# A hybrid attention and expert layer on one core: the last GpSimd work ahead of the experts is moved to VectorE, the gate vector's sums are moved later, and one hook of the experts one block on

## The chip, the cores and the metric

One core of one Trainium2 chip runs the whole layer in a single launch. The metric is the device time of the launch in microseconds (us), lower is better. The engines are named as in the profile: PE is TensorE, PEld its weight loads, DVE VectorE, ACT ScalarE, POOL GpSimd, SP SyncE. SP, POOL and ACT also issue DMA transfers.

## The reference

For 512 latent tokens of width 1024 (and 256 context tokens that are only read):

- A modulation vector is made from `c` with `w_ada`; its six parts of 1024 are shift, scale and gate of the attention half and of the expert half. The last part is the gate vector `g_m`.
- Two attention branches (grouped-query and differential) are computed, projected, merged with gates, and multiplied with `w_out`; `x = x + g_a * (...)`.
- `h = rmsnorm(x) * (1 + sc_m) + sh_m`. A router `h @ router_w + router_b` picks the top 4 of 32 experts for each token, with a softmax over the four.
- Each expert is `((up + 1) * gate * sigmoid(1.702 gate)) @ w_down + b_down` with clamped gate and up; `x = x + g_m * (weighted sum over the four)`.

All is in float32. Each expert has three weight matrices of 1024 x 1024, 4 MB each, so the experts read 403 MB.

## The kernel before

The code is written in program order, and a scheduler of the language may move instructions on each engine, except inside a `manual_schedule` block, where the engines that it lists keep the written order.

**Up to the experts.** After the attention, `out_products` multiplies with `w_oa` and `w_ob`, then the output projection with `w_out` runs as two column halves `n` by four token tiles `i`. After the second half of a tile, `x1[i]` is complete and the tile is routed: `scaled` multiplies it with the scale vector into `h2` (two halves of 128x512, on POOL), `routed` makes the reciprocal root `r`, completes `h2` on DVE and writes it to `h2d` in memory by DMA, and leaves three closures that are called later: `transposes`, `logits` (PE product with the router's weights, `lg`, the four largest `m`, the masks `gt`, `eq`, `mkb`) and `ranks` (how many earlier tokens chose the same expert, `rkm`). The product `py` has one PSUM buffer, so the logits of a tile wait until the ranks of the tile before have been read.

For tiles 2 and 3 all this is one chain with nothing else to do on PE: masks of tile 2, ranks, logits of tile 3, masks, ranks, then `one_hot` and `placed` (which tokens go to expert 0, their indices `ix`), then `gathered` (an indirect DMA that reads the rows of `h2d` into `xg`, issued by POOL), then the transposes of `xg` and the first expert's first product. Meanwhile the experts are sorted by their counts; that ends with `rkms` and `auxs`.

**Weights of the experts.** They come in 96 x 4 blocks of 1 MB (`fetch`), into 13 buffers; a block is fetched when a buffer is free (`used_up`). Blocks 8 to 11 are issued by POOL, the others by SP. Experts come in pairs: a large one (128 rows, three float32r products of split operands: `wh` is the rounded weight made by ACT, `wl` the rest, made by `wl = raw - wh`) and a small one (64 rows, plain float32, reading the raw block). `ahead(n)` makes up to `n` splits in advance; the kernel calls `ahead(3)` once before the experts. The subtractions of the first four splits were POOL's, all others DVE's.

**In the experts**, `product` goes through eight blocks `k` of 128 rows and calls the hooks that are given for a `k` first. `down(l, {1: input_of(l + 2), 4: act_of(l + 1)})` is the large expert's down product with two hooks: at `k` = 1 the next input is transposed, at `k` = 4 the small expert's activation `gS` is transposed; both through the one PSUM buffer `pt`. `aS`, its copy, is what the small expert's down product reads.

**The gate vector.** `ada_end` sums a vector's partial products over the 128 partitions: for each half of 512 one product with a matrix of ones and one ACT copy. `gm_bc` (tile `gm`) is first read when expert 0's output is scaled.

Of the kernel before, what the change touches and what calls it, by code (L numbers as in the profile page):

```python
# [8 lines left out]
FT = mybir.dt.float32  # L9
# [9 lines left out]
T, TC, D, E = 512, 256, 1024, 32  # L19
# [13 lines left out]
def tile_hybrid_block(  # L33
# [6 lines left out]
    PE, ACT, DVE, POOL, SP = nc.tensor, nc.scalar, nc.vector, nc.gpsimd, nc.sync  # L40
# [71 lines left out]
    acc = [acc2[:, j] for j in range(2)]  # L112
# [566 lines left out]
    def ada_end(p, a, scale):  # L679
        for n in range(2):  # L680
            ns = slice(n * 512, (n + 1) * 512)
            mm(p[:, ns], ones_f, a[:, ns], True, True)
            ACT.activation(a[:, ns], p[:, ns], AF.Copy, scale=scale)
# [205 lines left out]
            next(fill, None)  # L889
    opened["yp"] = open_pool("yp2", "right", stack=yst)  # L890
    yBH, yBL = halves("yB", yB, DVE)
    for a, scale in ((acc[0], 0.5), (acc[1], 1.0), (gm_bc, 1.0)):
        ada_end(ps.tile([128, D], FT, name="S", bufs=2), a, scale)


# [68 lines left out]
    for g in range(4):  # L964
        DVE.tensor_copy(diag[32 * g:32 * g + 32], marks[32 * g:32 * g + 32, 0, 32 * g:32 * g + 32])

    def expert_bias(j):
        b = braw[32 * j:32 * j + 32]
        if j == 1:
            DVE.tensor_scalar(b, b, 1.0, None, op0=OP.add)  # L970
        o = 64 * (j % 2)
        ACT.copy(bias[o:o + 32, j // 2], b)
        DVE.tensor_sub(bias[o + 32:o + 64, j // 2], b, bias[o:o + 32, j // 2])
# [4 lines left out]
    h2s, hTs = {}, {}  # L978
# [13 lines left out]
    def channels_x1(i, n):  # L992
        if n == 0:
            hTs[i] = fp.tile([128, NK, 128], FT, name="hT", bufs=2)
        pt = ps.tile([128, NK, 128], FT, name="pt", bufs=1)
        for k in range(4 * n, 4 * n + 4):
            PE.transpose(pt[:, k], x1[i][:, k * 128:(k + 1) * 128], ident)
        ACT.copy(hTs[i][:, 4 * n:4 * n + 4], pt[:, 4 * n:4 * n + 4])

    def scaled(i, n):  # L1000
        if n == 0:
            h2s[i] = fp.tile([128, D], FT, name="h2", bufs=2)
        ns = slice(n * 512, (n + 1) * 512)
        POOL.tensor_mul(h2s[i][:, ns], x1[i][:, ns], sc_bc[:, ns])

    def routed(i):

# [62 lines left out]
    for n in range(2):  # L1070
        ns = slice(n * 512, (n + 1) * 512)
        for i in range(4):
            p = ps.tile([128, D], FT, name=("pg", "pu")[i % 2], bufs=1)[:, ns]
            if n:
                channels_x1(i, 0)
            for k in range(NK):
                if n and i and k == 4:
                    stages[i - 1][0]()
                    if i > 1:
                        stages[i - 2][2]()  # L1080
                wh, wl = ws[k // 2][0][:, k % 2], ws[k // 2][1][:, k % 2]
                h, l = (t[k // 4][:, k % 4, i * 128:(i + 1) * 128] for t in (mTH, mTL))
                product3(p, h, l, wh, wl, k == 0, k == NK - 1)
            if n == 0 and i == 0:
                ada_end(ps.tile([128, D], FT, name="py", bufs=1), acc[2], 1.0)
                DVE.scalar_tensor_tensor(sc_bc, sc_bc, 1.0, nm, op0=OP.add, op1=OP.mult)
            if n == 0 and i == 3:
                ws = out_group(1)
            t = fp.tile([128, 512], FT, name="xt", bufs=2)
            DVE.tensor_mul(t, p, ga_bc[:, ns])  # L1090
            DVE.tensor_add(x1[i][:, ns], x1[i][:, ns], t)
            ACT.activation(t, x1[i][:, ns], AF.Square, scale=1.0 / 32.0, accum_out=sqs[:, i, n:n + 1])
            if n:
                scaled(i, 0)
                scaled(i, 1)
                stages.append(routed(i))
                if i:
                    stages[i - 1][1]()
            else:
                if i:  # L1100
                    expert_bias(i - 1)
                if i == 2:
                    router_weights()
# [47 lines left out]
    def ahead(n=BEFORE):  # L1151

        while len(split) < n and at_split[0] < len(to_split):
            i, a = to_split[at_split[0]]
            if i not in raws:
                return
            wh = xp.tile([128, D], FR, name="wh", bufs=BEFORE + 1)
            ACT.copy(wh, raws[i][:, a])  # L1158
            wl = xp.tile([128, D], FR, name="wl", bufs=BEFORE)
            (DVE if at_split[0] > 3 else POOL).tensor_sub(wl, raws[i][:, a], wh)  # L1160
            split[i, a] = wh, wl
            at_split[0] += 1
            if a:
                used_up(i)

    place, xg = {}, []
    for b, n in enumerate((D, 512)):
        t = xp.tile([128, n], FT, name=f"xg{b}")
        POOL.memset(t, 0.0)
        xg.append(t)  # L1170
    with tc.high_priority(300):
        stages[3][0]()
        stages[2][2]()
# [3 lines left out]
    def one_hot(e):  # L1177

        oh = xp.tile([128, 4, 128], FR if e else FT, name="oh", bufs=1)
        r, small = seq[e]  # L1180
        of = (rkms[:, :, r:r + 1] if e else rkm[:, :, 0:1]).to_broadcast([128, 4, 128])
        DVE.tensor_tensor(oh, rep(slots2 if small else slots1, 4), of, op=OP.is_equal)
        return oh

    def placed(e, oh):

        r, small = seq[e]
        pi = ps.tile([128, NK, 128], FT, name="pt", bufs=1)[:, 0, 0:4]
        ix = xp.tile([128, 1], I32, name="ix", bufs=6)
        w = xp.tile([128, 1], FT, name="wsl", bufs=6)  # L1190
        for i in range(4):
            mm(pi if e else pi[:, 0:2], oh[:, i], auxs[:, i, r] if e else aux[:, :, i, 0], i == 0, i == 3)
        if small:
            DVE.scalar_tensor_tensor(ix, pi[:, 0:1], 2.0, none, op0=OP.mult, op1=OP.add)
        else:
            DVE.tensor_scalar(ix, pi[:, 0:1], float(T), None, op0=OP.add)
        if e:
            DVE.reduce_sum(w, pi[:, 1:3], axis=AX)
        else:
            DVE.tensor_copy(w, pi[:, 1:2])  # L1200
        place[e] = ix, w
# [4 lines left out]
    def gathered(e):  # L1206
# [3 lines left out]
            in_offset=bass.IndirectOffsetOnAxis(ap=place[e][0][:, 0:1], axis=0),  # L1210
            bounds_check=(2 * T if small else T) - 1, oob_is_err=False)

    placed(0, one_hot(0))
    gathered(0)
    fetch(2)
    ahead(3)


    srt = ps.tile([128, D], FT, name="py", bufs=1)
# [30 lines left out]
    DVE.tensor_copy(bye, srt[:, 512:768].rearrange("p (a t) -> p a t", a=2))  # L1250
    for a in range(2):
        mm(srt[:, 768 + 128 * a:896 + 128 * a], bye[:, a], blocks.rearrange("p g e -> p (g e)"), True, True)
    DVE.tensor_copy(rkms, srt[:, 768:896].rearrange("p (i e) -> p i e", i=4))
    weights = srt[:, 896:1024].rearrange("p (i e) -> p i e", i=4)
    DVE.tensor_copy(auxs[:, :, :, 1], weights)
    DVE.tensor_sub(auxs[:, :, :, 2], weights, auxs[:, :, :, 1])
    for u in range(2):
        POOL.tensor_add(halvesr[:, u], blocks[:, 2 * u], blocks[:, 2 * u + 1])
    f1.close()


# [101 lines left out]
    def down(e, hooks={}):  # L1363
        p = result(e, 2)
        product(p, A[e], w_down, e, hooks)
        small = seq[e][1]
        y = ep.tile([128, p.shape[1]], FT, name=name_of(e))
        DVE.scalar_tensor_tensor(y, p, place[e][1], gm2 if small else gm_bc, op0=OP.mult, op1=OP.mult)
        POOL.indirect_dma_start(  # L1369
            out=by_place(out2, small), out_offset=bass.IndirectOffsetOnAxis(ap=place[e][0][:, 0:1], axis=0),  # L1370
            in_=y, in_offset=None, bounds_check=(2 * T if small else T) - 1, oob_is_err=False, compute_op=OP.add)

    def input_of(e):
        if e < E:
            X[e] = transposed(xg[e % 2], seq[e][1], "x")

    def act_of(e):
        A[e] = transposed(G[e], seq[e][1], "a")
# [29 lines left out]
    with tc.manual_schedule(engines={mybir.EngineType.PE, mybir.EngineType.Activation, mybir.EngineType.DVE}):  # L1408
        input_of(0)
        gate(0, {1: lambda: hot(1), 4: lambda: place_of(1)})  # L1410
        up(0, {2: lambda: hot(2), 3: lambda: input_of(1), 5: lambda: place_of(2)})
        gate(1, {1: lambda: hot(3), 3: lambda: place_of(3), 5: lambda: act_of(0)})
        up(1, {4: places_counted})
        down(0, {1: lambda: input_of(2), 4: lambda: act_of(1)})
        down(1, {3: lambda: input_of(3)})
        for l in range(2, E, 2):
            gate(l, {0: lambda: hot(l + 2), 3: lambda: place_of(l + 2), 4: lambda: hot(l + 3), 7: lambda: place_of(l + 3)})
            gate(l + 1)
            up(l)
            up(l + 1, {5: lambda: act_of(l)})  # L1420
            down(l, {1: lambda: input_of(l + 2), 4: lambda: act_of(l + 1)})
            down(l + 1, {3: lambda: input_of(l + 3)})
    ex.close()
    right.close()
# [126 lines left out]
```

## Time and profile before

| | us |
|---|---|
| median of three runs | 1627.09 (1625.44 to 1629.03) |
| the profiled execution | 1623.81 |
| its span in the trace | 1621.9 |
| PE busy in the span | 1537.2 (95%) |
| DVE busy | 1056.4 (65%) |
| POOL busy | 222.0 (14%) |

The span is what the trace covers; the 1.9 us beside it lie before the first and behind the last instruction. The median of the runs is 3.3 us above the profiled execution. Busy shares are means over stages with different limits, so the stages around the change are read one by one.

### The profile page before, as it was taken

To read this page: it belongs to the slowest core of one execution; us is meant where nothing else is said; L and a number is where in the kernel's file an instruction comes from. 1 tells how busy PE (TensorE), PEld (TensorE's weight loads), DVE (VectorE), ACT (ScalarE), POOL (GpSimd) and SP (SyncE) were. 2 spreads that over 40 slices of the span, in tenths; PEclk is the share of its full clock that TensorE was granted. 3 is DMA by queue.
4 is the path that set the end of the run, shared out by engine and by line. 5 is a ranking of instruction groups with operands and counts; after the bars stand their busy time and mean duration, and the time that the engine had idled before them with its cause. 6 is when DMAs were issued, how large, how long until landed. Compare 5 with 4: busy or idle time off the path is not lost. (4 is left out here: it accounts for less than half of the span.)

```text
span 1621.9 us, 20787 instructions
## 1 busy us (share of the span) xinstructions
PE 1537.2 (95%) x7303; PEld 1047.6 (65%) x7303; DVE 1056.4 (65%) x1668; ACT 754.1 (46%) x1051; POOL 222.0 (14%) x209
## 2 busy tenths in 40 slices
PE   7999999989999689999999999999999999999997
PEld 2778877778877564666666665656666565566564
DVE  6888888756877865566566575564565655656654
ACT  5668834256633243354445344443444434434442
POOL 3431000141001520010110110100101101001000
PEclk9999999999999879999999999999999999999999
DMA  8320055411365578999999999999999999999994
GB/s 315 91 66 27 27 169 166 146 53 40 105 194 208 220 290 356 405 403 421 406 405 423 402 410 408 394 413 395 398 412 387 411 402 387 418 389 395 411 401 153
DMA packets 102430, 483.43 MB, mean 298 GB/s; under 512 B 11393, under 2 KB 33082, under 8 KB 53170
## 3 DMA queue, kind: packets, MB, share of 16 engines
q1 hardware_dynamic: 91458, 453.71, 70.8%
q0 software_dynamic: 10720, 27.82, 6.0%
q8 instruction: 60, 0.98, 0.2%
q10 hardware_dynamic: 144, 0.52, 0.1%
q14 instruction: 48, 0.39, 0.1%
HBM read 473.62 MB, written 16.78 MB: 302 GB/s over the span
## 5 line engine op out<-in xcount | busy, mean ns | idle before, releaser
L1160 DVE TENSOR_TENSOR wl<-g,wh 128x1024 fp32r<-128x1024 f32 x110 | 130.7, 1222 | 61.0 <-ACT wh L1158 52.1
L1158 ACT CAST wh<-g 128x1024 fp32r<-128x1024 f32 x110 | 110.5, 1047 | 73.9 <-DMA g<-in_w_down_dram 31.9
L1160 DVE TENSOR_TENSOR wl<-raw,wh 128x1024 fp32r<-128x1024 f32 x86 | 103.9, 1239 | 53.4 <-ACT wh L1158 46.3
L1158 ACT CAST wh<-raw 128x1024 fp32r<-128x1024 f32 x90 | 90.9, 1047 | 62.8 <-DMA raw<-in_w_down_dram 23.8
L1160 DVE TENSOR_TENSOR wl<-x,wh 128x1024 fp32r<-128x1024 f32 x70 | 83.8, 1223 | 50.3 <-ACT wh L1158 42.0
L1158 ACT CAST wh<-x 128x1024 fp32r<-128x1024 f32 x70 | 71.2, 1048 | 70.0 <-DMA x<-in_w_down_dram 34.6
L1333 POOL CAST spread<-halvesr 128x128 fp32r<-128x128 f32 x16 | 4.6, 291 | 598.2 <-PE py L60 598.2
L60 PE MATMUL pg<-wh,xH 128*128 128x512 f32 x256 | 82.3, 403 | 0.0
L60 PE MATMUL pu<-wh,xH 128*128 128x512 f32 x256 | 81.8, 401 | 0.0
L60 PE MATMUL pg<-wh,xL 128*128 128x512 f32 x256 | 80.9, 397 | 0.0
L60 PE MATMUL pg<-wl,xH 128*128 128x512 f32 x256 | 80.6, 396 | 0.0
L60 PE MATMUL pu<-wh,xL 128*128 128x512 f32 x256 | 80.5, 395 | 0.0
L60 PE MATMUL pu<-wl,xH 128*128 128x512 f32 x256 | 80.5, 395 | 0.0
L564 DVE TENSOR_REDUCE mx<-S 128x1 f32<-128x768 f32 x64 | 60.4, 953 | 30.0 <-PE S L60 29.8
L567 ACT ACTIVATE P<-S,nb,rsq 128x768 f32<-128x768 f32 x64 | 63.6, 996 | 31.5 <-DVE nb L566 31.4
L1284 PE MATMUL py<-g,xS 128*64 128x512 f32 x328 | 77.6, 598 | 0.0
L163 ACT CAST wh<-wraw 128x1024 fp32r<-128x1024 f32 x54 | 56.8, 1055 | 40.7 <-DMA wraw<-in_w_in_dram 11.4
L1160 DVE TENSOR_TENSOR wl<-acc,wh 128x1024 fp32r<-128x1024 f32 x36 | 43.2, 1223 | 28.4 <-ACT wh L1158 23.9
L1160 DVE TENSOR_TENSOR wl<-y,wh 128x1024 fp32r<-128x1024 f32 x38 | 45.4, 1222 | 21.7 <-ACT wh L1158 18.1
L164 DVE TENSOR_TENSOR wl<-wraw,wh 128x1024 fp32r<-128x1024 f32 x39 | 47.9, 1232 | 16.9 <-ACT wh L163 16.8
L1284 PE MATMUL py<-raw,xS 128*64 128x512 f32 x248 | 58.7, 597 | 0.0
L60 PEld LDWEIGHTS pg<-wl,xH 128*128 128x128 f32 x256 | 48.3, 189 | 11.8
(466 smaller groups left out, 3734.4 us busy)
## 6 DMA issues: line engine op xcount, KB each, us to landing
g<-in_w_up_dram SPq DMA_DIRECT2D x42, 1024.0 KB, 18.6
g<-in_w_down_dram SPq DMA_DIRECT2D x38, 1024.0 KB, 19.7
g<-in_w_gate_dram SPq DMA_DIRECT2D x36, 1024.0 KB, 21.2
raw<-in_w_gate_dram SPq DMA_DIRECT2D x34, 1024.0 KB, 22.7
raw<-in_w_down_dram SPq DMA_DIRECT2D x29, 1024.0 KB, 17.7
raw<-in_w_up_dram SPq DMA_DIRECT2D x27, 1024.0 KB, 21.4
wraw<-in_w_ada_dram SPq DMA_DIRECT2D x40, 512.0 KB, 4.6
x<-in_w_gate_dram SPq DMA_DIRECT2D x20, 1024.0 KB, 23.5
```

The lines of the kernel that those rows point to most:

```text
L60: PE.matmul(o, l, r, start=start, stop=stop)
L163: ACT.copy(h, raw)
L164: (sub or DVE).tensor_sub(l, raw, h)
L564: DVE.reduce_max(mx, S, axis=AX)
L567: ACT.activation(P, S, AF.Exp, bias=nb, scale=rs, accum_out=sm)
L1158: ACT.copy(wh, raws[i][:, a])
L1160: (DVE if at_split[0] > 3 else POOL).tensor_sub(wl, raws[i][:, a], wh)
L1284: PE.matmul(p[64 * n:64 * n + 64], X[:, k], raws[i][:, a, n * 512:(n + 1) * 512], start=False, stop=True, skip_group_check=True)
L1333: POOL.tensor_copy(s[:, :, 1], halvesr[:, :, r:r + 1].to_broadcast([128, 2, SLOTS]))
```

## The change

The diff, whole but for the unchanged lines:

```
-    for a, scale in ((acc[0], 0.5), (acc[1], 1.0), (gm_bc, 1.0)):
+    for a, scale in ((acc[0], 0.5), (acc[1], 1.0)):
         ada_end(ps.tile([128, D], FT, name="S", bufs=2), a, scale)
...
+    xg = []
+    for b, n in enumerate((D, 512)):
+        t = rp.tile([128, n], FT, name=f"xg{b}")
+        POOL.memset(t, 0.0)
+        xg.append(t)
+
     def expert_bias(j):
...
-        POOL.tensor_mul(h2s[i][:, ns], x1[i][:, ns], sc_bc[:, ns])
+        (DVE if i == 3 and n else POOL).tensor_mul(h2s[i][:, ns], x1[i][:, ns], sc_bc[:, ns])
...
             if n:
                 channels_x1(i, 0)
+                scaled(i, 0)
...
             if n:
-                scaled(i, 0)
                 scaled(i, 1)
...
-            (DVE if at_split[0] > 3 else POOL).tensor_sub(wl, raws[i][:, a], wh)
+            DVE.tensor_sub(wl, raws[i][:, a], wh)
...
-    place, xg = {}, []
-    for b, n in enumerate((D, 512)):
-        t = xp.tile([128, n], FT, name=f"xg{b}")
-        POOL.memset(t, 0.0)
-        xg.append(t)
+    place = {}
...
+    ada_end(ps.tile([128, D], FT, name="pg", bufs=1), gm_bc, 1.0)
     placed(0, one_hot(0))
     gathered(0)
     fetch(2)
-    ahead(3)
...
-    DVE.tensor_copy(rkms, srt[:, 768:896].rearrange("p (i e) -> p i e", i=4))
-    weights = srt[:, 896:1024].rearrange("p (i e) -> p i e", i=4)
-    DVE.tensor_copy(auxs[:, :, :, 1], weights)
-    DVE.tensor_sub(auxs[:, :, :, 2], weights, auxs[:, :, :, 1])
     for u in range(2):
         POOL.tensor_add(halvesr[:, u], blocks[:, 2 * u], blocks[:, 2 * u + 1])
+    with tc.manual_schedule(engines={mybir.EngineType.Activation, mybir.EngineType.DVE}):
+        DVE.tensor_copy(rkms, srt[:, 768:896].rearrange("p (i e) -> p i e", i=4))
+        weights = srt[:, 896:1024].rearrange("p (i e) -> p i e", i=4)
+        DVE.tensor_copy(auxs[:, :, :, 1], weights)
+        DVE.tensor_sub(auxs[:, :, :, 2], weights, auxs[:, :, :, 1])
+        ahead(3)
...
-            down(l, {1: lambda: input_of(l + 2), 4: lambda: act_of(l + 1)})
+            down(l, {1: lambda: input_of(l + 2), 5: lambda: act_of(l + 1)})
```

What stands where in each engine's program follows from the scheduler. POOL's program from the last tiles' routing to the first expert, before (`h_5644` is `h2` of tile 3, `x_5087` its `x1`, `g_5849` and `acc` are buffers that take weight blocks):

```order
L1004 TENSOR_TENSOR h_5644<-x_5087,ac 128x512
L1015 DMA out_dram<-x_5087 128x1024
L1169 MEMSET xg_5697 128x1024
L1169 MEMSET xg_5699 128x512
L1160 TENSOR_TENSOR wl<-raw_5774,wh 128x1024 x2
L1160 TENSOR_TENSOR wl<-raw_5776,wh 128x1024
L1144 DMA g_5849<-in_w_down_dram 128x2048
L1208 DMA xg_5697<-h2d,ix 128x1024
L1258 TENSOR_TENSOR halvesr<-blocks 128x32 x2
L1144 DMA acc<-in_w_down_dram 128x2048
L1271 COPY gm_5862<-gm 64x512
```

and the same stretch of the change:

```order
L1021 DMA out_dram<-x_5082 128x1024
L1150 DMA g_5852<-in_w_down_dram 128x2048
L1150 DMA acc<-in_w_down_dram 128x2048
L1210 DMA xg_5120<-h2d,ix 128x1024
L1256 TENSOR_TENSOR halvesr<-blocks 128x32 x2
L1275 COPY gm_5865<-gm 64x512
```

The multiplication, the two memsets and the three subtractions are gone from this stretch, and the load of the block into `acc` stands ahead of the gather `xg<-h2d,ix` and no longer behind it. On DVE, where the sorting ends and the first expert's input is split (`xL` is the low part of that input), before:

```order
L1253 COPY rkms<-py 128x128
L1255 CAST auxs<-py 128x128
L1256 TENSOR_TENSOR auxs<-py,auxs 128x128
L1319 TENSOR_TENSOR xL<-pt,xH 128x512 x2
L1160 TENSOR_TENSOR wl<-raw_5835,wh 128x1024
```

and now:

```order
L1258 COPY rkms<-py 128x128
L1260 CAST auxs<-py 128x128
L1261 TENSOR_TENSOR auxs<-py,auxs 128x128
L1166 TENSOR_TENSOR wl<-raw_5774,wh 128x1024 x2
L1166 TENSOR_TENSOR wl<-raw_5776,wh 128x1024
L1323 TENSOR_TENSOR xL<-pt,xH 128x512 x2
L1166 TENSOR_TENSOR wl<-raw_5776,wh 128x1024
L1166 TENSOR_TENSOR wl<-raw_5838,wh 128x1024
```

The three subtractions of `ahead(3)` stand between `auxs` and `xL`, and the fourth behind `xL`. On DVE the scheduler has also put the completion of `h2` of tile 3 ahead of that tile's `lg`, where it stood behind it. On PE, between the logits of tile 2 and those of tile 3, the change reads:

```order
L60 MATMUL py<-rws,hT 128x32 x8
L60 MATMUL pg<-gm,ones_f 128x512
L1003 MATMUL pt<-marks,x_5082 128x128 x4
L60 LDWEIGHTS before
L60 MATMUL py<-mkb,before 128x32
L60 LDWEIGHTS ones_b
L60 MATMUL py<-mkb,ones_b 128x32
L60 LDWEIGHTS ones_b
L60 MATMUL py<-mkb,ones_b 128x32
L60 MATMUL pg<-gm,ones_f 128x512
L60 MATMUL py<-rws,hT 128x32 x8
```

The two rows `pg<-gm,ones_f` are new here; the rest stood in this order before. They stood among the products with `w_oa` and `w_ob`, and their PSUM tile was `S`.

## Rows read from the trace of the kernel before

**Rows 1.** Windows: us, busy (instructions) PE, PEld, DVE, ACT, POOL, clock, DMA share, GB/s

```profile
554.00:562.00 8.00, 0.00 (x0) 0.00 (x0) 8.00 (x2) 0.91 (x1) 8.00 (x6) 0.50 0.69 258
562.00:584.00 22.00, 13.67 (x58) 11.36 (x58) 13.12 (x65) 2.41 (x5) 5.58 (x12) 0.50 0.52 195
...
665.00:730.00 65.00, 65.00 (x298) 40.19 (x296) 40.79 (x43) 30.75 (x35) 6.32 (x5) 1.00 1.01 411
1120.00:1185.00 65.00, 62.27 (x281) 38.34 (x281) 37.56 (x40) 27.43 (x32) 5.59 (x5) 1.00 1.01 400
```

**Rows 2.** Timeline of DVE, 552 to 567 us: start, duration, line, operation, [idle before]

```profile
552.44 1.17 DVE L1033 TENSOR_SCALAR gt<-lg,m 128x32 f32<-128x32 f32 x1
553.54 8.94 DVE L1034 TENSOR_SCALAR eq<-lg,m 128x32 f32<-128x32 f32 x1
...
563.10 0.19 DVE L1041 TENSOR_TENSOR mkb<-gt,eq 128x32 bf16<-128x32 f32 x1
...
565.85 0.16 DVE L178 SCALAR_TENSOR_TENSOR r<-rs_t,r 128x1 f32<-128x1 f32 x1
```

**Rows 3.** Timeline of POOL, 552 to 564 us

```profile
554.12 1.43 POOL L1169 MEMSET xg<- 128x1024 f32 x2
555.50 6.94 POOL L1160 TENSOR_TENSOR wl<-raw,wh 128x1024 fp32r<-128x1024 f32 x3
```

**Rows 4.** Timeline of PE, 549 to 571 us

```profile
549.48 1.87 PE L60 MATMUL py<-rws,hT 128*128 128x32 f32 x16
552.38 0.63 PE L997 MATMUL pt<-marks,x 128*128 128x128 f32 x4 [1.03 <-DVE m L1029]
563.35 0.18 PE L60 MATMUL py<-mkb,before 128*128 128x32 bf16 x1 [10.34 <-DVE mkb L1041]
...
563.87 3.62 PE L60 MATMUL py<-rws,hT 128*128 128x32 f32 x16 [0.28 <-DVE rkm L1059]
```

**Rows 5.** Timeline of DVE, 567 to 582 us

```profile
567.70 1.28 DVE L1013 SCALAR_TENSOR_TENSOR h<-h,r,acc 128x1024 f32<-128x1024 f32 x1
568.89 0.19 DVE L1029 MAX8 m<-lg 128x8 f32<-128x32 f32 x1
...
570.15 0.19 DVE L1041 TENSOR_TENSOR mkb<-gt,eq 128x32 bf16<-128x32 f32 x1
...
579.43 0.39 DVE L1256 TENSOR_TENSOR auxs<-py,auxs 128x128 fp32r<-128x128 f32 x1
581.77 0.69 DVE L1319 TENSOR_TENSOR xL<-pt,xH 128x512 fp32r<-128x512 f32 x1 [1.95 <-ACT xH L1318]
```

**Rows 6.** Timeline of POOL, 574 to 583 us

```profile
574.60 1.11 POOL L1208 DMA_INDIRECT xg<-h2d,ix  x1 [11.63 <-DVE tmp L1243]
...
579.92 0.61 POOL L1271 COPY gm<-gm 64x512 f32<-64x512 f32 x1
...
581.06 0.53 POOL L1333 CAST spread<-halvesr 128x128 fp32r<-128x128 f32 x2
```

**Rows 7.** Timeline of DVE, 584 to 590 us

```profile
585.06 2.54 DVE L1160 TENSOR_TENSOR wl<-raw,wh 128x1024 fp32r<-128x1024 f32 x1 [1.26 <-ACT wh L1158]
...
588.12 1.21 DVE L1160 TENSOR_TENSOR wl<-raw,wh 128x1024 fp32r<-128x1024 f32 x1
```

**Rows 8.** Timeline of PE at the first expert's first product, 578 to 584 us

```profile
582.82 1.05 PE L60 MATMUL pg<-wh,xL 128*128 128x512 f32 x2
```

**Rows 9.** Timeline of PE, 466.5 to 468.4 us, one half of the gate vector

```profile
467.04 1.02 PE L60 MATMUL S<-gm,ones_f 128*128 128x512 f32 x2
```

**Rows 10.** Timeline of SP, 577 to 614 us

```profile
609.94 0.33 SPq L1144 DMA_DIRECT2D x<-in_w_down_dram  x1
```

**Rows 11.** Waits of PE, 612 us to the end: us in total, times, longest

```profile
PE pt L1308 <- DVE xL L1319: 15.1, 9, 1.7
```

**Rows 12.** Timeline of PE in one pair's two `down` products, 1074 to 1086 us

```profile
1078.36 0.72 PE L1308 MATMUL pt<-marks,gS 128*128 128x128 f32 x4 [1.68 <-DVE xL L1319]
...
1085.08 1.51 PE L1284 MATMUL py<-cL,aS 128*64 128x512 f32 x6
```

## Prediction

> **What bounds the kernel now.** Read the windows first [rows 1]. From 554 to 562 us PE does nothing, while DVE counts as busy for all 8.00 us with two instructions and POOL for 8.00 us with six. No other stretch of the kernel leaves PE idle that long. From 562 to 584 us PE is busy 13.67 of 22 us at a granted clock of 0.50, the lower level (1.2 GHz). In the experts there are two regimes. In 665 to 730 PE is busy all the time; in 1120 to 1185 it idles 2.7 us of 65, and the DMA engines are full in both (share 1.01, 411 and 400 GB/s). So the first half of the experts goes by PE, which eats the lead of the 13 buffers, and the second half by the stream of weights.
>
> The timelines tell what happened from 554 to 562. DVE's `eq`, a 128x32 comparison, starts at 553.54 and takes 8.94 us, where others on a 128x32 tile, such as `mkb`, take 0.19 [rows 2]. It ends at 562.48. POOL ran two memsets and three subtractions without a gap from 554.12 to 562.44 [rows 3]. So DVE got nothing done beside them, and was let go 0.04 us after the last one. PE's wait is the same time: 10.34 us before the ranks of tile 2, released by `mkb` [rows 4]. Behind it the 16 passes of tile 3's logits take 3.62 us, where those of tile 2 at the full clock took 1.87 [rows 4]. Nothing else runs on PE there; this chain leads to the first expert, so what it loses the kernel loses, if the weights' stream moves along.
>
> It does. The last fetch before the stream becomes continuous is issued at 609.94 [rows 10], into a buffer that expert 1's first product sets free. So the start of the stream follows PE, and the stream's end follows its start.
>
> **The change, part by part.**
>
> 1. *The stall.* `gt` begins at 552.44, some 0.1 us behind the search `m` for the four largest, and is itself stretched to 1.17 us [rows 2]. Now DVE first does POOL's multiplication: 0.69 us, from `xL`, an operation of the same shape [rows 5]. From the end of the search to the end of `mkb` tile 3, which nothing disturbed, needed 569.08 to 570.34, 1.26 us [rows 5]. So `mkb` of tile 2 ends at 552.34 + 0.69 + 1.26 = 554.3, say 554.4 with three small operations that are mixed in, instead of 563.29 [rows 2]. That is 8.9 us.
>
> 2. *The chain up to tile 3's search.* Now the ranks (0.2 us), then one half of the gate vector, which stands between ranks and logits: 1.02 us [rows 9], twice that at the half clock. Then the logits, 1.87 or 3.62. `r` ended 2.7 us behind `mkb` (566.01 against 563.29 [rows 2]), so at 557.1 now, and `h2`, which DVE now does before `lg`, takes 1.28 [rows 5] and ends at 558.4. With a full clock the logits end at 557.5, `lg` waits for `h2`, and the search behind it ends at about 558.8; with the half clock the logits end at 560.2 and the search at 560.6. Before, it ended at 569.08, since `h2` lay between `lg` and the search [rows 5]. Gain of 1 and 2 together: 8.5 to 10.3 us. Before the stall the clock was at its upper level, and PE now gets there with only some 1.5 us of idle time and with a half of the gate vector in the gap of 1.03 us before the last transposes [rows 4]; after a long idle stretch it was at the lower one. I take 9.6.
>
> 3. *The subtractions on DVE.* Three of them now stand between `auxs`, which ended at 579.82, and `xL`, which began at 581.77 after 1.95 us of waiting [rows 5]. Undisturbed one takes 1.21 us [rows 7], so three end at 583.5 and `xL` 0.69 later, at 584.2; PE's product with `xL` began at 582.82 [rows 8]. The loss is 1.4 us. The other end: POOL still has its copies of the gate vector and the casts of `spread` to do there, 579.92 to 581.6 [rows 6]. A subtraction that met one of POOL's took 2.54 us [rows 7], 1.3 more. If DVE gets nothing done until 581.6, that adds 1.8, so 3.2. If PE also stays at the lower clock through this wait for as long as the loss, up to another 1.3 us. I take 2.3 (bounds 1.4 and 4.5). The memsets of `xg`, moved to a time when PE is full, are hidden behind PE's products; uncovered they would cost their 1.43 us [rows 3].
>
> The Trainium skill, page "SBUF — State Buffer", section "SBUF: two separate sides", says that DVE and GpSimd share a port pair that is locked for a whole instruction, and that a DVE operation with two SBUF inputs is held only by a GpSimd operation that reads SBUF. By it the memsets of `spread` would not hold the subtractions and only the second copy and the casts would, about 1.2 us in all; by the row of `eq`, which passed no gap between six instructions, it is the whole 1.8. By that rule the sum would be 0.6 us better at its bad end.
>
> 4. *The gate vector.* The two products leave a stretch in which PE is the bound, 1.02 us each [rows 9]. The first half lies in a stretch where PE then waits for the merge anyway; other products are moved into its place. I take 1.2 of the 2.04 (bounds 0 and 2.0). The half that comes before tile 3's transposes is hidden in the wait of 1.03 us [rows 4]; without that cover it costs 1.02.
>
> 5. *The loads.* The block into `acc` is now issued before the gather, right behind `h2`, and the block into `g` some 9 us earlier. The DMA engines are idle for about half of 562 to 584 (share 0.52 [rows 1]), so the 2 MB, an estimated 2.5 us each at the 411 GB/s of [rows 1], fit in front of the gather. That was issued 5.5 us behind the search's end (574.60 [rows 6] against 569.08), so it comes some 6 us behind `h2` now. I put it at 0; if the gather stands behind both, it lands up to 4 us later. Buffer `raw0` comes free only behind its two subtractions, after `auxs`; the fetch behind it is for expert 1, whose first product comes after two of expert 0's, so 0.
>
> 6. *The hook.* Nine waits of up to 1.7 us, 15.1 in all, stand before the transposes of `gS` [rows 11]: `pt` is still read by `xL`. All lie in the second regime. From the end of these transposes to the small expert's product lie four blocks `k` in 6.0 us (1079.08 to 1085.08 [rows 12]), 1.4 to 1.5 each, so with the hook a block later the wait of 1.68 nearly goes. But PE then only waits longer for the next weights; the stream's bytes and rate stay. The last of these waits alone is worth something, since behind it PE runs to the end without one. I take 0.8 (bounds 0 and 1.7).
>
> **The sum.** -9.6 + 2.3 - 1.2 + 0 - 0.8 = -9.3 us, and 0.1 for an operation now in front of `one_hot`: -9.2. From the profiled execution's 1623.81 that gives 1614.6; its span 1621.9 would become about 1612.7. The median of the runs is 3.3 us above that execution, so I predict 1617.8. The bounds put together give -8.5 + 4.5 + 0.1 = -3.9 at the bad end and -10.3 + 1.4 - 2.0 - 1.7 + 0.1 = -12.5 at the good one: 1623.2 to 1614.6 on the median.
>
> **The rivals.**
>
> *The gather is late.* If the two loads and the write of `h2d` are still under way when the gather is issued, it lands up to 4 us later: -9.2 + 4 gives 1621.9. For it: the write of `h2d` and the load into `acc` now both wait for the same `h2`. Against it: 6 us lie between them and the gather, as worked out above. Chance 0.08.
>
> *The stream does not move.* If the end were set by the weights' bytes alone, from a start that the change leaves alone, an earlier first expert only makes PE wait longer: 1626 to 1627, and only the moved fetches count. The share of 1.01 in both windows [rows 1] speaks for it; the fetch at 609.94 that waits for PE [rows 10] speaks against. The Trainium skill, page "SBUF — State Buffer", section "A bandwidth-pool intuition that's wrong", holds that HBM is almost always the end-to-end bottleneck; by that rule this rival would be the likely one, though the trace agrees with it only from the middle of the experts on. Chance 0.06.
>
> *Slower: the small experts' activations come too late.* From the transposes of `gS` to the product that reads `aS` there were 6.7 us [rows 12]; the hook at 5 leaves 5.3. If the transposes (0.72) and ACT's copy, behind ACT's other work, need longer, PE waits in each of the 15 pairs of this loop. From 0.6 us a pair this eats the gain of 9.2; at 0.9 us a pair the time is 1617.8 + 13.5 = 1631. Against it: the copy itself is a 128x512 operation, which takes DVE 0.69 [rows 5], so some 3.9 us are left for what stands ahead of it on ACT. Chance 0.03.
>
> *The chain is not free of POOL.* POOL still issues two loads and the gather there. If issuing holds DVE as computing did, DVE loses 0.6 us for each of the first two and 1.1 for the gather [rows 6], 2.3 in all: 1620. That lies in the range. Chance 0.08. The forecast itself gets 0.75.
>
> **How the numbers follow.** The likeliest is 1617.8. The range is the bounds' 1614.6 to 1623.2, with about 1.5 us below for the spread of the medians: 1613 to 1623. It holds the forecast, the late gather and POOL's issuing. A measurement of this kernel tells 0.2%, 3.3 us, from no change. Faster by more: the forecast, the late gather and POOL's issuing, less their ends near 1623, 0.88. Within it: the stream's rival and those ends, 0.08. Slower: 0.04.
>
> **What would show it.** Right: no DVE instruction longer than 2 us between 551 and 575; PE's wait before tile 2's ranks at about 2 us; tile 3's logits below 2.5 us if the clock held; three `wl` of 1.2 us in front of `xL`, and a wait of PE of 1.4 to 3 us before the first product with `xL`; the first expert 7 to 9 us earlier; no waits before `gS`, but the aL waits or others of the second half longer, with the stream's share still 1.01. Wrong: a first expert that is earlier by 8 us with an end that is not; a gather that takes over 6 us; waits before `py<-...,aS` in every pair.

## The result, and the profile after

The changed kernel took 1617.25 us (median of 6 runs, 1613.8 to 1618.47) against 1627.87 us (6 runs of the kernel before on the same chip, 1623.64 to 1632.09). The ratio is 0.9937, 95% interval 0.9923 to 0.9951; the medians lie 10.6 us apart. The profiled execution took 1618.47 us with a span of 1616.7. That is only 5.3 us less than the profiled one of before, which was among the fastest of its kernel. The two traces are also shifted against each other in parts that the change leaves alone: tile 2's logits start at 552.61 instead of 549.48 [rows 4], although the gate vector's sums are gone from the time before them. Part of that is the granted clock: it is 0.98 in 150 to 250 us and 0.96 in 300 to 340, where before had 1.00, against 0.97 before in 250 to 300, where it is 1.00 now. So below, times around the chain are counted from the start of tile 2's logits, called T.

The windows of [rows 1], after the change (us, busy and instructions of PE, PEld, DVE, ACT, POOL, clock, DMA share, GB/s):

```profile
554.00:562.00 8.00, 5.01 (x32) 3.46 (x32) 7.58 (x41) 4.62 (x9) 2.12 (x4) 1.00 0.98 360
562.00:584.00 22.00, 13.35 (x54) 10.44 (x54) 15.04 (x39) 5.67 (x8) 6.54 (x9) 0.61 0.68 261
665.00:730.00 65.00, 65.00 (x296) 40.81 (x293) 38.68 (x41) 30.00 (x34) 7.20 (x5) 1.00 1.01 412
1120.00:1185.00 65.00, 63.09 (x281) 38.13 (x280) 38.27 (x40) 28.37 (x32) 6.39 (x5) 1.00 1.01 399
```

In the first window DVE now gets 41 instructions done instead of 2, and PE keeps its upper clock. DVE's timeline, to be read beside [rows 2]:

```profile
555.40 0.69 DVE L1010 TENSOR_TENSOR h<-x,ac 128x512 f32<-128x512 f32 x1
...
556.22 0.23 DVE L1040 TENSOR_SCALAR eq<-lg,m 128x32 f32<-128x32 f32 x1
...
557.14 0.19 DVE L1047 TENSOR_TENSOR mkb<-gt,eq 128x32 bf16<-128x32 f32 x1
...
559.45 1.28 DVE L1019 SCALAR_TENSOR_TENSOR h<-h,r,acc 128x1024 f32<-128x1024 f32 x1
...
560.93 0.20 DVE L1035 MAX8 m<-lg 128x8 f32<-128x32 f32 x1
```

`eq` takes 0.23 us instead of 8.94. PE's timeline, beside [rows 4, 8]:

```profile
555.51 0.63 PE L1003 MATMUL pt<-marks,x 128*128 128x128 f32 x4
557.39 0.18 PE L60 MATMUL py<-mkb,before 128*128 128x32 bf16 x1 [1.25 <-DVE mkb L1047]
...
557.52 1.13 PE L60 MATMUL pg<-gm,ones_f 128*128 128x512 f32 x2
558.49 1.87 PE L60 MATMUL py<-rws,hT 128*128 128x32 f32 x16
...
575.24 1.95 PE L1319 MATMUL pt<-marks,xg 128*128 128x128 f32 x8 [4.69 <-DMA xg<-h2d,ix]
...
578.95 1.05 PE L60 MATMUL pg<-wh,xL 128*128 128x512 f32 x2
```

The wait before the ranks is 1.25 us instead of 10.34 and tile 3's logits take 1.87 instead of 3.62. But a wait of 4.69 us has appeared behind the chain, for the gather, where before had 0.35. That row of before, and DVE's row of the indices `ix`, before and after:

```profile
579.11 1.96 PE L1315 MATMUL pt<-marks,xg 128*128 128x128 f32 x8 [0.35 <-DMA xg<-h2d,ix]
```

```profile
573.59 0.16 DVE L1196 TENSOR_SCALAR ix<-pt 128x1 int32<-128x1 f32 x1 [0.81 <-PE pt L60]
```

```profile
565.33 0.16 DVE L1198 TENSOR_SCALAR ix<-pt 128x1 int32<-128x1 f32 x1 [0.79 <-PE pt L60]
```

POOL's timeline:

```profile
556.18 0.53 POOL L1150 DMA_DIRECT2D g<-in_w_down_dram  x1
561.03 0.54 POOL L1150 DMA_DIRECT2D acc<-in_w_down_dram  x1 [4.31 <-DVE lg L1034]
570.66 1.10 POOL L1210 DMA_INDIRECT xg<-h2d,ix  x1 [9.10 <-PE py L60]
...
573.20 1.59 POOL L1275 COPY gm<-gm 64x512 f32<-64x512 f32 x1
574.75 0.41 POOL L1276 MEMSET spread<- 128x384 f32 x1
575.23 1.12 POOL L1275 COPY gm<-gm 64x512 f32<-64x512 f32 x1
```

The indices `ix` were written at 565.33, so the gather starts 5.3 us behind them; before it was 1.0 (573.59 to 574.60 [rows 6]). The name in its bracket, a product of PE, is only the event that came last. What it needs besides `ix` is tile 3's write of `h2d`, issued by ACT at 560.8. From the view of that tensor, ACT's row:

```profile
DMA to landing us min/median/max: 8.7/8.7/8.7
```

So the write landed at 569.5, and the gather followed 1.2 us later. DVE where the first expert's input is split, and PE's waits from 612 us on (us in total, times, longest), beside [rows 5] and [rows 11]:

```profile
571.49 4.38 DVE L1166 TENSOR_TENSOR wl<-raw,wh 128x1024 fp32r<-128x1024 f32 x3
577.89 0.69 DVE L1323 TENSOR_TENSOR xL<-pt,xH 128x512 fp32r<-128x512 f32 x1 [2.01 <-ACT xH L1322]
```

```profile
PE pu L60 <- DVE aL L1323: 3.6, 5, 0.8
PE pg L60 <- DVE aL L1323: 3.6, 5, 0.8
PE pt L1312 <- DVE xL L1323: 2.4, 9, 0.3
```

The three subtractions end at 575.87, before the gathered rows are even transposed, so `xL` does not wait for them. The waits before `gS` are down from 15.1 to 2.4 us; those for `aL` are up from 3.5 to 7.2.

### The profile page after: what moved, and what is told of

Its sections match the earlier page's. It is cut to its first block, busy times and chain, and to the rows that moved or that the text cites. A ratio compares the mean times of both kernels' runs of the same rounds, so it can differ in the third digit from the quotient of the medians.

```text
span 1616.7 us, 20768 instructions
## 1 busy us (share of the span) xinstructions
PE 1540.5 (95%) x7302; PEld 1044.5 (65%) x7303; DVE 1049.8 (65%) x1673; ACT 755.5 (47%) x1051; POOL 218.4 (14%) x204
## 5 line engine op out<-in xcount | busy, mean ns | idle before, releaser
L1166 DVE TENSOR_TENSOR wl<-g,wh 128x1024 fp32r<-128x1024 f32 x110 | 130.8, 1222 | 63.6 <-ACT wh L1164 54.8
L1166 DVE TENSOR_TENSOR wl<-raw,wh 128x1024 fp32r<-128x1024 f32 x90 | 108.0, 1231 | 59.8 <-ACT wh L1164 53.0
## 6 DMA issues: line engine op xcount, KB each, us to landing
raw<-in_w_down_dram SPq DMA_DIRECT2D x29, 1024.0 KB, 19.6
```

What stands on the lines that cost most here:

```text
L1166: DVE.tensor_sub(wl, raws[i][:, a], wh)
```

## The experiments

Eleven runs. "Gather" is the start of expert 0's gather, "first" PE's first product with `xL`, both behind T; "gather 1" is how long POOL's instruction for expert 1's gather takes; "expert 1" is that expert's first product (`py<-bias,spread`) behind T; "rest" is from there to the end of the span. The ratio is to the kernel before on the same chip.

| kernel | T | gather | first | gather 1 | expert 1 | rest | median | ratio (95%) |
|---|---|---|---|---|---|---|---|---|
| before | 549.48 | 25.12 | 33.34 | 1.84 | 57.93 | 1014.5 | | |
| changed | 552.61 | 18.05 | 26.34 | 1.06 | 51.08 | 1013.0 | 1617.25 | 0.9937 (0.9923-0.9951) |
| 1 memsets back | 550.02 | 16.49 | 25.29 | 1.06 | 50.75 | 1013.5 | 1616.16 | 0.9950 (0.9925-0.9976) |
| 2 subtractions back | 548.59 | 22.55 | 30.71 | 2.99 | 56.27 | 1013.5 | 1622.04 | 0.9977 (0.9966-0.9989) |
| 3 both back | 549.16 | 24.41 | 32.21 | 4.13 | 61.00 | 1012.9 | 1624.87 | 0.9991 (0.9978-1.0004) |
| 4 `acc` later | 549.75 | 15.90 | 24.93 | 4.11 | 53.11 | 1013.0 | 1616.38 | 0.9940 (0.9919-0.9961) |
| 5 two loads later | 550.09 | 13.47 | 23.85 | 1.07 | 49.25 | 1012.2 | 1613.49 | 0.9918 (0.9895-0.9941) |
| 6 and two subtractions | 547.38 | 13.77 | 21.60 | 5.27 | 53.54 | 1012.4 | 1617.26 | 0.9928 (0.9912-0.9945) |
| 7 hook at 4 | 550.81 | 18.29 | 26.43 | 1.06 | 51.12 | 1015.6 | 1619.73 | 0.9947 (0.9931-0.9963) |
| 8 gate vector back | 552.97 | 18.29 | 28.43 | 2.99 | 53.45 | 1012.8 | 1620.44 | 0.9951 (0.9935-0.9967) |
| 9 and a turn for POOL | 550.32 | 13.54 | 21.73 | 1.07 | 47.43 | 1012.8 | 1612.34 | 0.9915 (0.9897-0.9933) |
| 10 one subtraction later | 550.40 | 13.32 | 22.37 | 5.27 | 53.62 | 1012.6 | 1616.67 | 0.9928 (0.9903-0.9952) |
| 11 changed, again | 548.58 | 18.35 | 27.12 | 2.99 | 52.26 | 1013.3 | 1615.97 | 0.9947 (0.9926-0.9968) |

The interval of a ratio is about 2 us to either side or more, so effects of 1 or 2 us are read from the traces. Each trace is one execution: the two of the changed kernel (changed and 11) differ by 0.8 us at the first product and by 1.2 at expert 1, so a difference of that size between single traces of two kernels is only a hint.

### 1 to 3: the stall put back in parts

Run 1 takes the move of the memsets of `xg` back, so that they stand behind tile 2's routing again; run 2 gives the first three subtractions back to POOL; run 3 does both. The edit of run 2, which run 3 has too:

```
-            DVE.tensor_sub(wl, raws[i][:, a], wh)
+            (DVE if at_split[0] > 2 else POOL).tensor_sub(wl, raws[i][:, a], wh)
...
     fetch(2)
+    ahead(3)
...
-        ahead(3)
```

> The changed kernel with one part undone: the two memsets of the gather's buffers stand on GpSimd again between the writes of tile 2 and the loads, in the stretch in which VectorE searches the masks of tile 2. The subtractions stay on VectorE. Theory (any GpSimd instruction holds VectorE there): the two took 1.43 us before, so gt, eq or another of the mask operations takes up to 1.4 us, mkb ends 2.5 to 3.3 us behind the search instead of 1.85, everything behind it moves by 0.7 to 1.4 us, and the time is about 1618 to 1619. Rival (what counts is whether the GpSimd instruction reads SBUF; a memset does not): no mask operation above 0.3 us, mkb 1.85 us behind the search, 1617.3. The Trainium skill, page SBUF — State Buffer, section SBUF: two separate sides, states the rival's rule for VectorE operations with two SBUF inputs.

> The changed kernel with the other part undone: the first three subtractions of the experts' weights stand on GpSimd again, in front of the gather; the memsets stay early. Theory (GpSimd's arithmetic holds VectorE): one mask operation of tile 2 lasts 5 to 7.5 us, TensorE idles some 8 us before tile 2's ranks, tile 3's logits take 3.6 us at the lower clock, the first expert starts 5 to 7 us later than in the changed kernel as counted from tile 2's logits, and the time is about 1623 to 1625. Rival (the end is set by the weights' stream, whatever the first expert does): the same stall in the trace but a time of 1617 to 1618.

> The changed kernel with memsets and subtractions back on GpSimd; of the change only the gate vector's later sums, the order on VectorE and the hook are left. Theory: eq takes about 8.9 us as before, the first expert is about as late behind tile 2's logits as before (31 us), and what is left of the gain is the gate vector's 1.2 and the hook's 0.8 us: about 1626. Rival (the order on VectorE, with h2 of tile 3 completed before its search, made much of the gain): 1620 to 1623.

In run 1 `gt` and `eq` last as long as the memsets; DVE's rows, then POOL's:

```profile
553.48 1.58 DVE L1033 TENSOR_SCALAR gt<-lg,m 128x32 f32<-128x32 f32 x1
553.62 1.46 DVE L1034 TENSOR_SCALAR eq<-lg,m 128x32 f32<-128x32 f32 x1
```

```profile
553.59 1.43 POOL L1169 MEMSET xg<- 128x1024 f32 x2
```

`mkb` comes 3.0 us behind the search (552.88 to 555.85) instead of 1.7 (555.48 to 557.14) in the changed kernel: the memsets hold these comparisons, as my theory has it, and the rival's rule does not hold for them. No end came later, though: the write of `h2d` was issued 1.3 us later behind T but took 6.2 us instead of 8.7, and the gather waited for it either way. So the 1.3 us went into a wait that was there already; why the write took less time is not shown. In run 2 one `gt` is held through all three subtractions; DVE's row, then POOL's:

```profile
552.05 7.13 DVE L1039 TENSOR_SCALAR gt<-lg,m 128x32 f32<-128x32 f32 x1
```

```profile
552.19 6.95 POOL L1166 TENSOR_TENSOR wl<-raw,wh 128x1024 fp32r<-128x1024 f32 x3
```

The first product with `xL` comes 4.4 us later than in the changed kernel, a little less than the 5 to 7 expected, and expert 1 5.2 us. The ratio gives 1623.3 us of 1627, and its interval lies wholly above the changed kernel's, so the rival is out. With both back (run 3) `gt` and `eq` last 8.48 and 8.36 us, the first product is within 1.1 us of that of the kernel before, and the interval of the ratio includes 1. Expert 1 is even 3.1 us later, behind a gather of 4.13 us that PE waited 3.2 us for (runs 6 and 9 tell more of it). The order on DVE, the rival of run 3, made no more than the 1.1.

### 4 and 5: the loads ahead of the gather

In run 4 the block into `acc`, in run 5 also the one into `g2` (`g` in the rows) is bound to the gather's indices by a one-column write, so that it is issued behind the gather:

```
+            if i in (9, 11):
+                DVE.tensor_copy(raws[i][:, 0, 0:1], place[0][1])
             (POOL if 8 <= i < 12 else SP).dma_start(raws[i], weights_of(*order[i]))
```

(Run 4 has `(11,)`.)

> The changed kernel with one load moved: the 1 MB block into acc is issued behind the gather and no longer in front of it. In the changed kernel the gather was issued 5.2 us after its indices were ready, 1.2 us behind the landing of tile 3's h2d write and 0.3 behind that of the acc block. Theory A (the gather waits for tile 3's write, which lands late because the loads issued before it fill the DMA engines): the write lands 0 to 2 us earlier, the gather still follows it by about 1.2 us, the first expert comes 0 to 2 us earlier, 1615.5 to 1617.3. Theory B (the gather waits for the acc block itself): the gather follows the write by 0.3 us or less, first expert at least 1 us earlier. Theory C (it waits for neither): the gather stays where it is.

> The changed kernel with two loads moved: the blocks into g2 and acc (1 MB each) are issued behind the gather, where the change had put both in front of it. Theory A (the gather waits for tile 3's write, late behind full DMA engines): the write of 0.5 MB lands 3 to 6 us earlier, the gather is issued within 1.5 us of its indices and lands 3 to 5 us earlier. Then the three subtractions, so far hidden behind the late gather, show: xL waits for them 1.4 to 2.5 us. Net 1.5 to 3.5 us earlier first expert, time 1614 to 1616. Rival (the write is slow by itself, 8.2 to 8.7 us whatever else is under way): no change, 1617.3.

In run 4 the gather comes 2.1 us earlier and the first product 1.4; expert 1 still comes 2.0 us later, behind a gather of 4.11 us that PE waited 2.5 us for. That the changed kernel's gather waited for the write and not for the block in `acc` (theory A, not B) is shown by run 1: there the gather starts at 566.51, 0.8 us behind the write (issued 559.5, 6.2 us) but ahead of the block's landing (issued 559.74, 8.4 us). In runs 7 and 8 it starts 1.2 us behind the write, as in the changed kernel, and in run 8 0.2 us ahead of the block's landing. In run 5 the write takes 4.2 us, and the gather starts 0.5 us behind its indices. The DMA engines' share, in the columns of the windows above, in run 5 and then in the changed kernel:

```profile
558.00:563.00 5.00, 2.26 (x16) 2.07 (x15) 3.62 (x22) 0.32 (x1) 0.00 (x0) 0.83 0.71 285
```

```profile
558.00:564.00 6.00, 3.11 (x29) 2.56 (x27) 5.37 (x30) 1.32 (x3) 0.54 (x1) 1.00 0.99 388
```

The share was 0.99 and is 0.71. With both loads ahead of it the write took 6.2 to 9.0 us (8.7 in the changed kernel, 6.2, 9.0 and 6.6 in runs 1, 7 and 8), with none ahead 4.1 to 4.5 (runs 5, 6 and 10). So the two loads, which filled the engines, made the write slow. Now the subtractions show in run 5; DVE, then PE:

```profile
569.29 4.00 DVE L1168 TENSOR_TENSOR wl<-raw,wh 128x1024 fp32r<-128x1024 f32 x3
573.21 0.68 DVE L1325 TENSOR_TENSOR xL<-pt,xH 128x512 fp32r<-128x512 f32 x1
```

```profile
573.94 0.73 PE L60 MATMUL pg<-wh,xL 128*128 128x512 f32 x2 [2.11 <-DVE xL L1325]
```

The first product is 2.5 us earlier than in the changed kernel.

### 6, 9 and 10: the subtractions behind `xL`

Run 6 leaves ACT's roundings where they are and defers the second and third subtraction, run 10 only the third:

```
-        ahead(3)
+        ahead(1)
+        ahead(3, late)
...
         input_of(0)
+        for low in late:
+            low()
         gate(0, ...
```

(`ahead` appends the subtraction to `late`, if given, instead of issuing it. Run 10 has `ahead(2)`.)

> The kernel before this one (both loads behind the gather) with two of the three subtractions moved behind xL on VectorE; ScalarE's roundings stay early. Theory: the first expert's product with xL starts as early as the gather allows, 3 to 5 us earlier than in the changed kernel, and the end follows: 1612.5 to 1614.5. Rival 1 (the subtractions are then late for the product with wl, which needs one of 1.2 us for each 1.4 us of TensorE): TensorE waits up to 1.2 us for wl, 1614 to 1615. Rival 2 (the end no longer follows the first expert): 1616.5 to 1617.5.

In run 6 the first product came as early as hoped, 4.7 us before that of the changed kernel, and yet expert 1 came 2.5 us later. DVE's rows, POOL's, PE's, and a window:

```profile
578.80 2.35 DVE L1172 TENSOR_TENSOR wl<-cL,wh 128x1024 fp32r<-128x1024 f32 x2
581.07 2.35 DVE L1172 TENSOR_TENSOR wl<-g,wh 128x1024 fp32r<-128x1024 f32 x2
584.30 2.36 DVE L1172 TENSOR_TENSOR wl<-g,wh 128x1024 fp32r<-128x1024 f32 x2 [0.88 <-ACT wh L1166]
```

```profile
579.09 5.27 POOL L1219 DMA_INDIRECT xg<-h2d,ix  x1 [9.66 <-DVE wsl L1209]
```

```profile
590.48 1.10 PE L1322 MATMUL pt<-marks,xg 128*128 128x128 f32 x4 [4.04 <-DMA xg<-h2d,ix]
```

```profile
588.00:592.00 4.00, 1.52 (x6) 1.45 (x7) 0.40 (x1) 0.38 (x1) 0.00 (x0) 0.64 1.02 425
```

Expert 1's gather took POOL 5.27 us instead of 1.06. It began while DVE, in arrears, subtracted without a gap from 578.80 to 583.42, and ended at 584.36, in DVE's first gap. PE then waited 4.04 us, and the clock fell. It looks like the stall of [rows 2, 3] with the roles exchanged. None of the theories had it. Run 9 tests it by giving POOL a turn:

```
             gathered(e)
+            if e == 1:
+                t = [ep.tile([128, 1], FT, name=f"turn{j}") for j in range(2)]
+                POOL.tensor_copy(t[0], place[e][1])
+                DVE.tensor_copy(t[1], t[0])
```

> The kernel with loads and two subtractions later, and a pause on VectorE behind expert 1's indices: GpSimd copies 128 numbers after its gather, VectorE copies them once more, and only then goes on subtracting. Without it the gather of expert 1 took GpSimd 5.27 us instead of 1.06, while VectorE subtracted without a gap from 578.80 to 583.43; it landed 11.25 us after its start, and TensorE waited 4.0 us. Theory (VectorE's unbroken subtractions hold GpSimd's issue): the gather takes about 1.1 us again, lands within 6.5 us, TensorE waits 0 to 1 us there and up to 1 us for a late wl; expert 1 starts 3 to 4 us earlier, and the time is 2.5 to 4 us below that kernel's. Rival (the gather was slow because the two loads were still under way on the same queue): it still takes over 3 us, and nothing is gained.

> The kernel with both loads later, with one subtraction instead of two behind xL. Theory: the first product with xL comes between the two kernels, some 1 us earlier than with none later; VectorE is behind by one subtraction less, but still without gaps when expert 1's gather is issued, so that the gather takes 3 to 5 us and most of it is lost again: within 1 us of the kernel with two subtractions later. Rival (one subtraction less of arrears leaves a gap): gather 1.1 us, about 1 us better than with none later.

Run 9's rows of DVE, POOL and PE:

```profile
583.22 0.15 DVE L1407 COPY turn<-turn 128x1 f32<-128x1 f32 x1 [1.51 <-POOL turn L1406]
```

```profile
581.92 1.07 POOL L1219 DMA_INDIRECT xg<-h2d,ix  x1 [9.61 <-DVE wsl L1209]
```

```profile
589.73 0.72 PE L1322 MATMUL pt<-marks,xg 128*128 128x128 f32 x4 [0.44 <-DMA xg<-h2d,ix]
```

With DVE idle for 1.51 us the gather takes 1.07 us, PE waits 0.44, and expert 1 comes 6.1 us earlier than in run 6: 3.6 by the wait, the rest mostly by the clock that no longer falls (between 592 and 596 us it was 0.50 in run 6 and is 1.00 in run 9). The two loads are issued as in run 6, so the rival is out. The times say less: 0.9915 against 0.9928, with intervals that overlap. Run 10 came out as its theory said, with a gather of 5.27 us, a little over the 3 to 5.

In the Trainium skill, page "SBUF — State Buffer", section "SBUF: two separate sides", a warning says that GpSimd cannot write the descriptors of a DMA that it issues while DVE runs an operation in a two-port mode, such as a float32 copy within SBUF. The subtractions here are of another kind, with two inputs in SBUF, which the warning does not name; runs 6 and 10 against run 9 show that the gather waits for them too, 5.27 against 1.07 us. Whether it is the descriptors that wait, no run here shows.

### 7 and 8: the hook and the gate vector put back

```
-            down(l, {1: lambda: input_of(l + 2), 5: lambda: act_of(l + 1)})
+            down(l, {1: lambda: input_of(l + 2), 4: lambda: act_of(l + 1)})
```

> The changed kernel with the hook of the experts back at block 4. Theory (the stream of weights sets the second half, so a wait taken away there comes back elsewhere): the waits before the transposes of gS return, 15 us in all, and the time rises by 0 to 1.7 us, 1617.3 to 1619; in the first half, where TensorE is the bound, each pair is up to 0.2 us longer, some 10 pairs, so up to 2 us. Rival (the waits are real losses): 15 us less 1.7 for the last, at least 5 us, 1622 or more.

Run 7's wait for `xL` is back (15.0 us, 9 times), and its rest is 1015.6; the kernel before has 1014.5, and the eleven traces with the hook at 5 have 1012.2 to 1013.5, mean 1012.9. So the hook is worth about 2.1 us (1.0 to 3.4), of 12.6 us of waits taken away. The times (1.6 us, within the intervals) don't add to that: the worth of the hook rests on two traces with it at 4 and eleven with it at 5. Run 8:

```
-    for a, scale in ((acc[0], 0.5), (acc[1], 1.0)):
+    for a, scale in ((acc[0], 0.5), (acc[1], 1.0), (gm_bc, 1.0)):
...
-    ada_end(ps.tile([128, D], FT, name="pg", bufs=1), gm_bc, 1.0)
```

> The changed kernel with the gate vector's sums back among the products with w_ob. Theory: these two products cost 1.2 us there (the step in the difference of the two traces), and nothing where the change put them: 1618.5. Rival (at the new place they fill gaps that cost the clock, so that taking them away drops the clock in tile 3's logits): the logits take 3.6 instead of 1.87 us and the time is 1619.5 to 1620.5.

```profile
557.75 0.19 PE L60 MATMUL py<-mkb,before 128*128 128x32 bf16 x1 [1.25 <-DVE mkb L1047]
...
558.32 3.62 PE L60 MATMUL py<-rws,hT 128*128 128x32 f32 x16 [0.33 <-DVE rkm L1065]
```

```profile
556.00:558.00 2.00, 0.74 (x7) 0.45 (x6) 1.99 (x16) 1.95 (x5) 1.05 (x2) 0.83 0.99 348
558.00:562.00 4.00, 3.62 (x16) 3.52 (x17) 1.58 (x13) 0.27 (x1) 0.00 (x0) 0.50 0.98 367
```

Both the theory and the rival hold. At the old place the sums cost 1.8 us in the mean: from the first `yv<-ones_f` product behind 425 us to the first `py<-ac,ones_f`, PE takes 64.0 us before and 64.7 in run 8, but 61.3 to 63.6, mean 62.6, in the eleven traces with the sums at the new place. And without them at the new place PE's clock falls to 0.50 ahead of tile 3's logits, which take 3.62 us; the search of tile 3 ends 10.6 us behind T instead of 8.5. The first product comes 2.1 us later too, but not by that alone: the gather starts only 0.2 us later, since it waited for the write either way, and lands 6.4 us behind its start instead of 4.4. How much of that is the clock's is not shown.

## Why the prediction was right, point by point

The number was 1617.8 (the sum itself gives 1617.9); the time is 1617.25. It was right as a sum, but partly by luck, because terms that were off cancelled: a late gather cost 4.3 us that the sum did not have, and a chain that gained 1.5 us more, subtractions that cost nothing, and a hook and a gate vector that gave more made up for it.

1. **The stall and the chain** (-9.6, bounds -8.5 to -10.3). Runs 2 and 3 show the mechanism. The size was larger: from T to the end of tile 3's search it was 19.6 us before (569.08) and is 8.5 (561.13), a gain of 11.1, over the bound. The clock held, and `r` and `h2` were ready 0.8 us sooner than worked out. Without the gate vector there the clock falls (run 8), but with it the clock does not hold in every execution either: where the subtractions' stall is gone, the logits took 1.87 us in six traces and 2.06, 2.28 and 2.69 in runs 4, 1 and 11, the last of them the same kernel.
2. **The gather, at 0** (step 5). This is the term that failed: 4.3 us of the gain were lost in front of the gather. I had the DMA engines half idle there, but that share (0.52 [rows 1]) was a mean over 22 us at the old times; with the chain earlier, the write met engines 0.99 full. So the rival of the late gather, with a chance of 0.08, came about, at its full price of 4 us, though not its time of 1621.9, since other terms gave more. Run 5 takes it away.
3. **The subtractions** (+2.3, bounds 1.4 to 4.5) cost nothing in the changed kernel, since the late gather hid them; the wait of 1.4 to 3 us before the first product with `xL` did not come. Run 5, where it isn't late, has the price: 2.1 us. Together 1 to 3 come to -7.0 at the first product (33.34 to 26.34) where -7.2 was predicted. The three took 4.38 us instead of the 3.49 of run 8, where they met nothing of POOL's but a memset. Here they met POOL's additions for `halvesr` and its copies, 1.59 and 1.12 us instead of 0.60; the memset of `spread` between them took its 0.41. So they took turns, and neither waited for the whole of the other's work. That fits the rule of the Trainium skill, page "SBUF — State Buffer", section "SBUF: two separate sides", as the prediction weighed it, that the memsets don't hold these subtractions; run 1 shows that memsets do hold `gt` and `eq`.
4. **The gate vector** (-1.2, bounds 0 to -2.0) measured -1.8 at the old place (0.4 to 3.4 between single traces). That it also keeps the clock stood in the chain's two ends, 1.8 us apart (search at 558.8 or 560.6); run 8 has 2.0 us at the end of that search.
5. **The hook** (-0.8, bounds 0 to -1.7) measured about -2.1, over the bound. Some of it lies in the first half, for which the prediction had nothing: from 640 to 1000 us the changed kernel's lead over the kernel before grows from 3.7 to 4.6 us, that of run 7 only from 5.5 to 5.6. The list of waits shows none before `gS` there, but the starts of PE's rows show where the gain lies: from the last product ahead of the transposes of `gS` to the first behind them it is 1.03 us before (697.07 to 698.10) and 0.85 now (694.77 to 695.62), 0.18 us less, and the lead grows by as much in each of five pairs. What takes that time is open.
6. **The stream moves along.** Over thirteen traces expert 1's start lies between 47.4 and 61.0 us behind T, and the rest stays within 3.4 us, 1.3 with the hook at 5. So the end follows expert 1 in full, and the rival by which bytes alone set it is out.
7. **aS too late**, the slower rival: no such wait is in the list. POOL's issuing did not hold DVE either; no DVE instruction between tile 2's search and the subtractions lasts over 1.28 us.

The terms -7.0, -1.8 and -2.1 come to -10.9; measured were -10.6. Each is read from single traces that spread by 1 us or more, so that they meet this closely is partly luck.

## What to carry to other kernels

When a chain gets shorter, look at what its DMAs will meet at their new times: the share of the DMA engines has to be read in the stretch where the transfer will lie, not where it lay. Big loads that nobody needs soon are issued behind the small transfer that somebody waits for. Where DVE and GpSimd can hold each other, a run of DVE work without a gap can delay a DMA that GpSimd issues; a deliberate pause of 1.5 us brought expert 1 forward by 6.1 us in run 9's trace, though the times of runs 6 and 9 don't tell the two apart.

Run 9 has the lowest ratio, 0.9915 to the kernel before, 3.6 us below the changed kernel on the same chip. The two intervals overlap a little, and run 5 with 0.9918 is not told apart from it; that expert 1 comes 3.7 to 4.8 us earlier in its trace than in the changed kernel's two is what speaks for it.

## What the runs showed that was not expected

- The changed kernel differs between executions at expert 1's gather: 1.06 us in one trace, 2.99 in run 11, for which 1.1 was expected and where PE then waited 1.1 us. In all eight traces in which this instruction took longer than 1.1 us it ends 0.93 to 0.94 us behind the end of a subtraction: in the kernel before behind the one that was running as it began, in runs 2, 8 and 11 behind the second, in 3 and 4 the third, in 6 and 10 the fourth. In five of them DVE paused behind that subtraction, for 0.06 to 0.90 us, but in the kernel before and in runs 2 and 8 the next one follows at once. Run 2's rows, DVE's and then POOL's:

```profile
587.05 2.35 DVE L1166 TENSOR_TENSOR wl<-cL,wh 128x1024 fp32r<-128x1024 f32 x2
589.33 1.23 DVE L1166 TENSOR_TENSOR wl<-g,wh 128x1024 fp32r<-128x1024 f32 x1
```

```profile
587.35 2.99 POOL L1210 DMA_INDIRECT xg<-h2d,ix  x1 [8.49 <-DVE wsl L1200]
```

So POOL waits for whole subtractions and a pause is not always needed, though the long one of run 9 kept the wait away. What decides for how many it waits is not shown.

- Two products of 1.1 us in gaps of a chain kept PE's clock at its upper level through 1.87 us of logits in six of the nine traces without the subtractions' stall; in run 8, without the two products, PE was at 0.50 there. In run 11 they kept it only in part: the clock was 0.66 from 554 to 558 us and the logits took 2.69.
